# A two-layer hybrid trunk on one core: from the first layer's last tiles through latents and attention, one list of steps in place of the scheduler's order

## The chip, the cores and the metric

One core of a Trainium2 chip runs the whole program in one launch. The time is the device time in microseconds (us), the median of several runs; before the change it is 2141.66 us, from three runs of 2141.5 to 2142.57. One execution is also profiled; its records give every instruction's start and length on the engines: PE (TensorE, matmul and transpose), DVE (VectorE), ACT (ScalarE), POOL (GpSimd) and SP (SyncE, which here issues the loads). Lines such as L170 are lines of the kernel before.

## The reference

The input is a sequence of 1024 tokens by 1024 features in float32. Layer 0 is a gated short convolution with an MLP of 4096, layer 1 is multi-head latent attention with an MLP. Between them a shared key and value side is built from the residual stream. Cut to what this case touches:

```python
def shared_kv(x, c_act, kv_ada_w, kv_ada_b, kv_norm_g, kv_a_w, kv_a_norm_g, kv_b_w, cos, sin):
    ...
    hkv = modulate(rmsnorm(x, kv_norm_g), shift, scale)
    kv_a = hkv @ kv_a_w                                   # 1024 -> 256 + 64
    c_kv = rmsnorm(kv_a[..., :KV_LORA], kv_a_norm_g)
    k_pe = apply_rope(kv_a[..., KV_LORA:], cos, sin)
    kv = (c_kv @ kv_b_w).reshape(B, S, N_HEADS, QK_NOPE + V_HEAD)
    return kv[..., :QK_NOPE], kv[..., QK_NOPE:], k_pe

def mla_mixer(h, q_a_w, q_a_norm_g, q_b_w, o_w, k_nope, v, k_pe, cos, sin):
    q = (rmsnorm(h @ q_a_w, q_a_norm_g) @ q_b_w).reshape(B, S, N_HEADS, QK_NOPE + QK_ROPE)
    ...
    for i in range(S // Q_BLOCK):                         # 8 blocks of 128 queries
        s = q_nope . k_nope + q_pe . k_pe                 # scaled, 8 heads, keys up to the block's end
        s = where(k_chunk <= q_chunk, s, min)             # chunks of 64
        p = softmax(s)
        outs.append(p @ v)
    return concatenate(outs) @ o_w
```

Every layer is wrapped as `x = x + g * rmsnorm(y)`, with shifts, scales and gates that are sums over `silu(c)` times columns of `ada_w`.

## The kernel before

Matrix products are made from two parts of each float32 operand, a high part in a rounded format and the remainder, so that each product is three matmuls (`mm`, L167 to L170). An operand is split by a copy on ACT (L173) and a subtraction on DVE (L174). Token tiles are 128 tokens by 1024 features, and there are eight; feature blocks are 128, and there are eight (`KD`); "halves" are 512 tokens. PSUM is shared by pairs of `mm` and `tp` tiles of one bank and two `big` tiles of two banks.

The stretch that the change touches goes in these steps.

1. *The last rows of the first layer's down projection* (`down`, L889). For each token tile `t` 24 matmuls write a `big` tile, and `Seam.tile` (L298) adds it to `y` (L309), takes the root of the sum of its squares (`squares`, L255 to L257, on ACT), scales it (L315), adds it to the residual tile (L316), stores that, takes its squares too, and at the next tile `flush` writes the normalised tile (L295). For tiles 5 to 7 `front` issues two transposed feature blocks each.
2. *The first products of the query latent* (`first_block`, L632): per feature block three groups of three matmuls, and between them the remaining steps of the transposes (`h_steps`, L475: four transposes L484, an eviction with scale and shift on ACT L486, a split on DVE L490 and L491).
3. *The latents* (`latent`, L1300): for queries (384 features) and keys (256), by halves: copy out of PSUM (L1311), squares (L1312), their sum over features as a product with a matrix of ones (L1315), root (L1316), a reciprocal over 512 columns (L1317), scaling (L1319), a split (L1320, L1321). `rotary_keys` makes the rotated key of 64 features. The second half's steps and the key's steps are issued within the products of the part ahead of them.
4. *Attention* over eight heads. For a head: `keys` (L1424, L1425), `queries` (L1430, L1431), for two heads together `rotary` (L1440, L1441) and `values` (L1454, L1455); then for each of eight blocks of queries, from 7 down to 0, `scores`: five matmuls per 512 keys (L1471), a mask by `memset` (L1472), the maximum (L1474), the exponential with its sum (L1477), and the division (`end`, L1481, L1482). `turn` transposes probabilities (L1497) and splits them (L1500, L1501); `mul` multiplies them by the values; the result is stored (L1532, L1533). The loop over heads gives the program's order: the scores of the next block beside the preparation of the next head and the products of the head before. Loads of a head's weights and five steps of the background sums (`run_bg`, L195, weights by weights) stand at the head's start.

The order in which an engine runs its instructions is fixed when the program is built. Without further words a scheduler chooses it from the program's order and its own estimate of durations. `pinned` (L109) adds edges that make the engines keep the written order for what stands within it. Steps 1 and 2 are pinned in part, attention is not. In the other two places where a down projection meets an up projection, the order of all steps is already a written list, `ORDER` (L45 to L55), which `first_pairs` (L652) follows; its entries are names of steps with their tile or block.

Four `raw` tiles of 512 KB take all loads of weights in turn; a load waits until its tile's last reader is done.

Of the kernel before, what the change touches and what calls it, by code (L numbers as in the profile page):

```python
# [8 lines left out]
F32 = mybir.dt.float32  # L9
# [24 lines left out]
MASKED = -(2.0 ** 127)  # L34
# [17 lines left out]
P5_3 p6_0 nt2d p4_1 p3_2 D9_3 nS2 p6_3 nS3 p7_3 ns2a o6 p4_3 nt3a ns2d p5_3 nt3d o5 o4 p3_3 o3 o7  # L52
""".split()
# [8 lines left out]
def trunk_kernel(ctx: ExitStack, tc: tile.TileContext, x, c, ada_w, ada_b, norm_g, conv_in_w, conv_w,  # L62
# [92 lines left out]
    eps_d = cp.tile([P, 1], F32, name="eps_d")  # L155
    nc.vector.memset(eps_d, D * EPS)
    eps_1 = cp.tile([P, 1], F32, name="eps_1")
    nc.vector.memset(eps_1, EPS)
# [109 lines left out]
    class Seam:  # L268
# [4 lines left out]
        def __init__(self, nx, ys, gmb, xsrc, xdst, last=False):  # L273
            self.nx, self.ys, self.gmb, self.xsrc, self.xdst, self.last = nx, ys, gmb, xsrc, xdst, last
            self.rest, self.backs, self.xr = None, [], {}
# [6 lines left out]
        def front(self, steps, n):  # L282
            for _ in range(min(n, len(steps))):
                f, b = steps.pop(0)
                f()
                self.backs.append(b)

        def back(self):
            while self.backs:
                self.backs.pop(0)()  # L290

        def flush(self):
            if self.rest is not None:
                y, xr, ss = self.rest
                nc.scalar.activation(y, xr, AF.Copy, scale=rroot(ss))  # L295
            self.rest = None

        def tile(self, t, p_, steps):  # L298
# [9 lines left out]
            with pinned():  # L308
                nc.vector.tensor_tensor(y, y, p_, op=ALU.add)  # L309
                self.back()  # L310
                ss = squares(self.nx, y)
                self.flush()
                if t >= 5:
                    self.front(steps, 2)
                nc.vector.scalar_tensor_tensor(y, y, rroot(ss), self.gmb, op0=ALU.mult, op1=ALU.mult)  # L315
                nc.vector.tensor_tensor(xr, xr, y, op=ALU.add)  # L316
                nc.scalar.dma_start(self.xdst[t * P:(t + 1) * P, :], xr)
                if not self.last:
                    self.rest = (y, xr, squares(self.nx, xr))
# [4 lines left out]
        def acts(self, first):  # L324


            acts, ss, sx, rs = {}, {}, {first - 1: self.rest[2]}, {}
# [44 lines left out]
        def finish(self, t, y, xr, p_):  # L372
# [3 lines left out]
            ss, rt, eps = [small(), small()], small(), small()  # L376
            with pinned():
# [3 lines left out]
                nc.vector.tensor_tensor(eps, eps_d, ss[0], op=ALU.add)  # L381
                for sl in halves_:
                    nc.vector.tensor_tensor(self.gmb[:, sl], self.gmb[:, sl], y[:, sl], op=ALU.mult)
                nc.scalar.activation(rt, ss[1], AF.Sqrt, bias=eps)
# [89 lines left out]

    def h_steps(tp, ys, half, key, dst):  # L475

        hi, lo = dst
        s1, sh = vtile["s" + key], vtile["h" + key]
        tts = {}

        def step(k):
            p_ = tp_ps()
            for t in range(4):
                nc.tensor.transpose(p_[:, t * P:(t + 1) * P], ys[half * 4 + t][:, k * P:(k + 1) * P], ident)  # L484
            tt = tp.tile([P, HALF], F32, tag="tt", name=nm("tt"), bufs=2)
            nc.scalar.activation(tt, p_, AF.Identity, scale=s1[:, k:k + 1], bias=sh[:, k:k + 1])  # L486
            tts[k] = tt

        def split(k):
            nc.vector.tensor_copy(hi[:, k, :], tts[k])  # L490
            nc.vector.tensor_tensor(lo[:, k, :], tts[k], hi[:, k, :].bitcast(F32), op=ALU.subtract)  # L491

        return [(lambda k=k: step(k), lambda k=k: split(k)) for k in range(KD)]
# [137 lines left out]

    def first_block(seam, steps0, steps1, ws, h):  # L632

        ps_ = [mm_ps(), mm_ps(), big_ps()[:, :HALF]]
        for k in range(KD):
            with pinned():
                for p_, w in zip(ps_, ws):
                    mm(p_, (w[0][:, k, :], w[1][:, k, :]), (h[0][:, k, :], h[1][:, k, :]), k == 0, k == KD - 1)
                if k == 0:
# [1036 lines left out]
```

## Time and profile before

| | us |
|---|---|
| median of three runs | 2141.66 |
| the profiled execution | 2144.59 |
| its span, first to last instruction | 2142.8 |
| list's stretch: product of tile 5 to the last product of attention | 1004.9 to 1420.5 |
| of it up to the last latent | 1004.9 to 1117.0 |
| of it attention | 1117.0 to 1420.5 |

The granted clock of TensorE is 0.996 on average. Rows of the stretches give busy time of each engine, with the number of instructions in brackets. In the rows of the timeline stand start, length, engine, line, operation and tiles, with the idle time ahead of it and what ended that in square brackets. Rows "A <- B: total, times, longest" say how long A's engine stood idle until B. Rows of groups have "busy, mean ns | idle before". Two matmuls in a row overlap in their records, since a record lasts until its result is written.

### The profile page before, as it was taken

The numbers are of one execution on the slowest core, as the hardware profiler recorded it, in microseconds if no ns is written. First come the engines' busy times: TensorE is split into PE (matmuls) and PEld (weight loads), VectorE is DVE, ScalarE is ACT, GpSimd is POOL, SyncE is SP. The second block draws the span as 40 slices with busy tenths as digits, with TensorE's granted clock in tenths as the row PEclk, the third lists the DMA queues.
The fourth block names the chain that finished last, engine by engine and source line by source line (L and its number), as shares of the span: only waits on it lengthen the run. The fifth ranks groups of instructions, "written<-read, shape, count | busy, mean of one in ns | idle before, by whom it ended". The sixth has DMA issues, their size and how long they took to land.

```text
span 2142.8 us, 25254 instructions
## 1 busy us (share of the span) xinstructions
PE 2083.0 (97%) x9638; PEld 1715.1 (80%) x9638; DVE 1532.3 (72%) x2066; ACT 1060.5 (49%) x1512; POOL 4.0 (0%) x8
## 2 busy tenths in 40 slices
PE   5999999999999999999899999999999999999998
PEld 4888888888888878888777878877888888888887
DVE  5877776977665668876788877766977665558556
ACT  4533353845444434344665555564845444444342
POOL 0000000000000000000000000000000000000000
PEclk9999999999999999999999999999999999999999
DMA  8344454466443976465214231043455543853343
GB/s 245 95 147 146 131 200 136 133 192 215 157 152 131 326 230 226 151 210 178 81 59 124 78 106 44 26 149 132 129 184 184 183 166 134 300 191 122 98 147 138
DMA packets 242336, 330.85 MB, mean 154 GB/s; under 512 B 18630, under 2 KB 143907, under 8 KB 242215
## 3 DMA queue, kind: packets, MB, share of 16 engines
q1 hardware_dynamic: 204328, 248.57, 37.2%
q10 hardware_dynamic: 37886, 80.67, 10.0%
q8 instruction: 76, 1.25, 0.2%
q14 instruction: 46, 0.37, 0.0%
HBM read 248.45 MB, written 80.74 MB: 154 GB/s over the span
## 4 chain that ended last, share of the span: by engine, by line
PE 75%; DVE 12%; ACT 6%; DMA 5%; issue 2%; ACTq 0%; SPq 0%; DVEq 0%
PE one L170 40%; PE mm L170 19%; PE tp L170 7%; PE big L170 3%; ACT junk L255 2%; DMA raw<-in_ada_w_dram 2%; PE big L1471 2%; DVE y L315 1%; DVE raw L316 1%; DVE acc L195 1%; PE tp L1497 1%; DVE small L1474 1%; DVE y L309 1%; DVE pt L1501 1%; ACT small L257 1%
## 5 line engine op out<-in xcount | busy, mean ns | idle before, releaser
L170 PE MATMUL one<-slot,uphi 128*128 128x512 f32 x1240 | 381.9, 389 | 0.0
L170 PEld LDWEIGHTS one<-slot,uphi 128*128 128x128 f32 x1240 | 232.8, 188 | 48.7 <-issue 0.5
L170 PE MATMUL big<-slot 128*128 128x512 f32 x1152 | 267.6, 392 | 0.9 <-DVE slot L174 0.6
L170 PEld LDWEIGHTS big<-slot 128*128 128x128 f32 x1152 | 216.0, 189 | 47.7 <-ACT y L924 1.0
L170 PE MATMUL one<-slot,uplo 128*128 128x512 f32 x620 | 243.0, 392 | 1.6 <-DVE y L584 1.6
L173 ACT ACTIVATE ring<-w 128x1024 fp32r<-128x1024 f32 x98 | 103.8, 1059 | 267.1 <-PE tp L170 145.7
L170 PE MATMUL one<-ring,ring 128*128 128x512 f32 x1008 | 229.5, 389 | 0.3 <-DVE ring L174 0.3
L170 PEld LDWEIGHTS one<-ring,ring 128*128 128x128 f32 x1008 | 189.2, 188 | 40.0 <-DVE ring L174 0.7
L174 DVE TENSOR_TENSOR ring<-w,ring 128x1024 fp32r<-128x1024 f32 x98 | 119.8, 1222 | 122.8 <-ACT ring L173 122.6
L174 DVE TENSOR_TENSOR uplo<-raw,uphi 128x1024 fp32r<-128x1024 f32 x117 | 142.7, 1222 | 79.1 <-ACT uphi L173 79.0
L173 ACT ACTIVATE uphi<-raw 128x1024 fp32r<-128x1024 f32 x117 | 123.7, 1059 | 136.1 <-PE one L170 77.4
L170 PE MATMUL mm<-ring,ring 128*128 128x512 f32 x672 | 163.1, 391 | 2.4 <-DVE ring L174 2.4
L170 PE MATMUL tp<-ring,ring 128*128 128x512 f32 x672 | 161.8, 389 | 0.0
L170 PE MATMUL mm<-slot,uphi 128*128 128x512 f32 x504 | 157.9, 394 | 0.5 <-DVE slot L430 0.5
L170 PEld LDWEIGHTS mm<-ring,ring 128*128 128x128 f32 x672 | 125.6, 188 | 29.7 <-DVE ring L174 3.5
L170 PEld LDWEIGHTS tp<-ring,ring 128*128 128x128 f32 x672 | 126.1, 188 | 26.2
L170 PEld LDWEIGHTS one<-slot,uplo 128*128 128x128 f32 x620 | 116.4, 188 | 26.5 <-DVE y L584 2.4
L195 DVE SCALAR_TENSOR_TENSOR acc<-raw,csil,acc 128x1024 f32<-128x1024 f32 x88 | 112.4, 1277 | 35.1 <-DMA raw<-in_ada_w_dram 32.5
L174 DVE TENSOR_TENSOR ring<-raw,ring 128x1024 fp32r<-128x1024 f32 x98 | 119.3, 1218 | 10.7 <-ACT ring L173 10.7
L170 PE MATMUL one<-slot,s 128*128 128x512 f32 x468 | 114.0, 393 | 0.7 <-DVE s L174 0.7
L170 PEld LDWEIGHTS mm<-slot,uphi 128*128 128x128 f32 x504 | 94.8, 189 | 21.1 <-issue 1.4
L582 ACT ACTIVATE y<-one 128x512 f32<-128x512 f32 x62 | 36.7, 592 | 143.5 <-PE one L170 114.3
(272 smaller groups left out, 3487.0 us busy)
## 6 DMA issues: line engine op xcount, KB each, us to landing
ha<-y ACTq DMA_DIRECT2D x196, 256.0 KB, 3.0
raw<-ha SPq DMA_DIRECT2D x98, 512.0 KB, 4.3
raw<-in_ada_w_dram SPq DMA_DIRECT2D x80, 512.0 KB, 4.4
raw<-in_mlp_up_w_dram SPq DMA_DIRECT2D x70, 512.0 KB, 4.9
w<-in_mlp_down_w_dram SPq DMA_DIRECT2D x56, 512.0 KB, 4.8
raw<-hd SPq DMA_DIRECT2D x24, 512.0 KB, 4.3
xs<-raw ACTq DMA_DIRECT2D x24, 512.0 KB, 3.1
raw<-xs SPq DMA_DIRECT2D x24, 512.0 KB, 4.2
```

Source lines behind the costliest of these rows:

```text
L170: nc.tensor.matmul(out_, lhs[a], rhs[b], start=first and i == 0, stop=last and i == 2, skip_group_check=more)
L173: nc.scalar.activation(hi, src, AF.Copy)
L174: nc.vector.tensor_tensor(lo, src, hi.bitcast(F32), op=ALU.subtract)
L195: nc.vector.scalar_tensor_tensor(acc, raw, s, acc, op0=ALU.mult, op1=ALU.add)
L255: nc.scalar.activation(junk, src, AF.Square, accum_out=ss)
L257: nc.scalar.activation(rt, ss, AF.Sqrt, bias=eps_d)
L309: nc.vector.tensor_tensor(y, y, p_, op=ALU.add)
L315: nc.vector.scalar_tensor_tensor(y, y, rroot(ss), self.gmb, op0=ALU.mult, op1=ALU.mult)
L316: nc.vector.tensor_tensor(xr, xr, y, op=ALU.add)
L582: nc.scalar.activation(dst, x_, AF.Copy)
L1471: nc.tensor.matmul(o_, a, m_, start=j == 0, stop=j == 4)
L1474: nc.vector.tensor_reduce(mx, sp[:, :n], AX.X, ALU.max, negate=True)
```

## The change

A second list, `ATTENTION`, of 1121 entries names every step from the product of tile 5 (`mm5`) to the last output of head 7 (`o7.0`). A letter or two stand for the kind of step, then head (or pair of heads), half, and block. Its first part (up to the first entry that belongs to attention, `bB0`) runs in a pinned context over the engines, the rest in a pinned context over the engines and one over SP, which holds the loads `lq` (query weights), `lk` (key and value weights) and `bl` (rows for background sums). Steps that were one function become several entries: `scores` is `S` (matmuls), `m` (mask and maximum), `e` (exponential), `t` (division); `turn` and `mul` are `T`, `u`, `w` and `P`; keys `K`, `Ka`, `Kd`; and so on.

Beside the order these things change:

- The query latent isn't normalised. Its high part is a scaled copy straight from PSUM, and its squares' sums go, by token, through four matmuls of one column into a column `rsq` for each tile of tokens, `(root of 192 * mean square + eps)` and its reciprocal on eight columns. `rsq` is the scale of the exponential, and the maximum is multiplied by it: one more DVE instruction of one column for each score tile. The scale by 1/sqrt(192) goes with it, so queries' and rotary steps lose their constant factor.
- The key latent's sums go by token too, and its reciprocal root is spread over partitions by four transposes for each half.
- In `Seam.tile` the addition to the residual tile, its store and its squares move from their own tile to the next one, under the wait for that tile's squares. This holds for all three projections that are followed by another one; the last one keeps its order.
- `MASKED` becomes -(2^120). The functions `front`, `back`, `h_steps`, `first_block`, `latent`, `rotated`, `Values` and the loop over heads go.

```diff
+ATTENTION = """
+mm5 tr0_0 tr0_1 add5 tu0_0 mm6 tu0_1 sq5 sp0_1 stt5 rc4 xad5 pre4 mm7 add6 sqx5 sp0_0 sq6 rc5 pre5 stt6 dma5 xad6 tr0_2
+tr0_3 tu0_2 f0 add7 tu0_3 sqx6 sp0_2 tr0_4 mul7 tr0_5 sq7 f1 sp0_3 tu0_5 stt7 dma6 tr0_6 tu0_4 f2 sp0_4 sqx7 rc6 sp0_5 tr0_7
+pre6 f3 rc7 dma7 pre7 tu0_6 f4 tu0_7 sp0_6 sp0_7 tr1_0 tr1_1 tu1_0 f5 tu1_1 sp1_0 sp1_1 tr1_2 tr1_3 tu1_2 f6 tu1_3 sp1_2
...
+Kd2.1 P0.0.1 t1.3 m1.6 P0.0.2 Q2.1 o0.0 Rl1.1.1 e1.6 bs0.6 S1.2 Qa2.1 t1.6 Q2.0 Qd2.1 m1.2 bs0.7 T1.1.0 e1.2 T1.1.1 Qa2.0
+V1.3 t1.2 u1.1.1 Qd2.0 u1.1.0 w1.1.1 S1.0 Va1.3 w1.1.0 K2.0 lq3 m1.0 Vd1.3 e1.0 T1.1.2 Ka2.0 T1.1.3 t1.0 u1.1.2 P1.1.0 Kd2.0
+u1.1.3 P1.1.1 w1.1.2 w1.1.3 V1.1 T1.1.4 Va1.1 P1.1.2 u1.1.4 Vd1.1 P1.1.3 w1.1.4 S2.4 P1.1.4 m2.4 T1.1.5 T1.1.6 S1.1 u1.1.5
...
+P7.1.3 e7.0 w7.1.5 T7.1.6 t7.0 P7.1.4 u7.1.6 T7.0.0 w7.1.6 P7.1.5 u7.0.0 T7.0.1 w7.0.0 P7.1.6 u7.0.1 T7.0.2 P7.0.0 o7.1
+w7.0.1 u7.0.2 P7.0.1 w7.0.2 P7.0.2 o7.0
+""".split()
...
         def flush(self):
             if self.rest is not None:
-                y, xr, ss = self.rest
-                nc.scalar.activation(y, xr, AF.Copy, scale=rroot(ss))
+                t, y, xr = self.rest
+                nc.vector.tensor_tensor(xr, xr, y, op=ALU.add)
+                nc.scalar.dma_start(self.xdst[t * P:(t + 1) * P, :], xr)
+                self.ss = None if self.last else squares(self.nx, xr)
+
+        def tail(self):
+            if self.rest is not None and not self.last:
+                t, y, xr = self.rest
+                nc.scalar.activation(y, xr, AF.Copy, scale=rroot(self.ss))
             self.rest = None
...
                 nc.vector.tensor_tensor(y, y, p_, op=ALU.add)
-                self.back()
                 ss = squares(self.nx, y)
+                if not self.last:
+                    self.flush()
+                nc.vector.scalar_tensor_tensor(y, y, rroot(ss), self.gmb, op0=ALU.mult, op1=ALU.mult)
+                self.tail()
+                self.rest = (t, y, xr)
+                if self.last:
+                    self.flush()
...
+        def token_sums(p_, sq):
+            for t in range(4):
+                nc.tensor.matmul(p_[:, t:t + 1], sq[:, t * P:(t + 1) * P], ones[:, 0:1], start=True, stop=True)
...
+        def k_spread(hf):
+            for t in range(4):
+                nc.tensor.transpose(t_["vs", hf][:, HALF + t * P:HALF + (t + 1) * P], t_["vr", hf][:, t:t + 1].to_broadcast([P, P]), ident)
...
+        def maxima(h, i):
+            n = (i + 1) * P
+            sp, mx = ps_["S", h, i], small()
+            nc.vector.memset(sp[:CHUNK, n - CHUNK:n], MASKED)
+            nc.vector.tensor_reduce(mx, sp[:, :n], AX.X, ALU.max, negate=True)
+            nc.vector.tensor_tensor(mx, mx, rsq[:, i:i + 1], op=ALU.mult)
+            stats[h, i] = mx
+
+        def exponentials(h, i):
...
+            nc.scalar.activation(pts[h, i], ps_.pop(("S", h, i))[:, :n], AF.Exp, scale=rsq[:, i:i + 1], bias=stats[h, i], accum_out=l_)
...
+    with pinned():
+        for name in ATTENTION[:n]:
+            acts[name]()
...
+    attention(acts, t_["qw"], t_["kw"])
+    with pinned(), pinned([mybir.EngineType.SP]):
+        for name in ATTENTION[n:]:
+            acts[name]()
```

776 lines of the change are left out of this document (440 added, 336 removed).

## The prediction

> **What bounds the kernel now.** I read the page's head, then busy time by stretch, then the timeline of TensorE (PE) inside the stretch that the change rewrites, then who waits for whom there.
>
> ```profile
> span 2142.8 us, 25254 instructions
> PE 2083.0 (97%) x9638; PEld 1715.1 (80%) x9638; DVE 1532.3 (72%) x2066; ACT 1060.5 (49%) x1512; POOL 4.0 (0%) x8
> ```
>
> PE bounds the whole. But "busy" hides waits: a matmul's record is longer than the distance to the next one, so a short wait vanishes in the overlap. The distances between starts show the true price.
>
> ```profile
> 943.00 2.88 PE L170 MATMUL mm<-ring,ring 128*128 128x512 f32 x12
> 945.72 2.88 PE L170 MATMUL tp<-ring,ring 128*128 128x512 f32 x12
> ...
> 1390.68 0.34 PE L1471 MATMUL big<-slot,r 128*128 128x384 f32 x1
> 1390.86 0.34 PE L1471 MATMUL big<-k,q 128*128 128x384 f32 x1
> ...
> 1394.93 0.28 PE L1471 MATMUL big<-slot,r 128*128 128x256 f32 x1
> 1395.05 0.28 PE L1471 MATMUL big<-k,q 128*128 128x256 f32 x1
> ...
> 1396.74 0.28 PE L1471 MATMUL big<-k,q 128*128 128x128 f32 x1
> 1396.85 0.27 PE L1471 MATMUL big<-slot,r 128*128 128x128 f32 x1
> ```
>
> Twelve matmuls of 512 columns take 2.72 us from start to start: 0.227 each. 384 columns cost 0.18, 256 cost 0.12, 128 cost 0.11. I use 0.11 for one column too, and about 0.5 per record for the f32 products with `ones`.
>
> ```profile
> 1004.90:1117.00 112.10, 105.18 (x500) 83.46 (x501) 87.61 (x124) 70.90 (x115) 0.00 (x0) 0.98 0.25 81
> 1117.00:1420.50 303.50, 289.67 (x1605) 239.72 (x1604) 238.86 (x476) 171.58 (x340) 0.96 (x1) 0.99 0.25 78
> 1115.00:1157.00 42.00, 36.88 (x188) 29.47 (x187) 40.32 (x63) 25.72 (x44) 0.96 (x1) 1.00 0.43 132
> 1224.80:1299.20 74.40, 71.50 (x408) 60.11 (x406) 59.53 (x120) 41.18 (x84) 0.00 (x0) 1.00 0.27 86
> 1299.20:1371.50 72.30, 70.95 (x408) 59.93 (x406) 51.59 (x111) 41.13 (x84) 0.00 (x0) 1.00 0.11 37
> ```
>
> (Columns: stretch, its length, then PE, weight loads, DVE, ACT, POOL busy with counts, PE clock, DMA share, GB/s.) The first row runs from the product of tile 5 of the first layer's down projection, the list's first entry, to the last latent; the second is attention; then come attention's start and two pairs of heads.
>
> PE's own work follows from the code's counts. Latents: 72 matmuls for tiles 5 to 7, 144 for queries, 96 and 48 for keys and values and the rotary key, all of 512 columns: 360 x 0.227 = 81.7; 128 transposes x 0.11 = 14.1; 8 `ones` records x 0.5 = 4.0. Together 99.8, so 12.3 of 112.1 us is excess. Attention: 696 of 512 columns (K 96, Q 144, rotary 72, scores 240, values' products 144) 158.0; 128 of 384 23.0; 320 of 256 38.4; 416 of 128 45.8; 32 one-column records 3.5; 4 `ones` records 2.0; and 11 of the next projection 2.5. Together 273.2 and 1607 matmuls, beside x1605 in the row. Excess 30.3. **What the change can win is these 42.6 us**, 10% of a stretch in which PE calls itself 95% busy. DVE is the second bound: 239 of 303.5 in attention (79%), 96% in its first 42 us.
>
> **The change part by part.** (a) *The hand-over from the down projection to the latents.* The old order issues two steps of eight transposes behind tiles 5 to 7 and waits:
>
> ```profile
> 1027.05 1.93 PE L484 MATMUL tp<-cs,y 128*128 128x128 f32 x8 [3.39 <-ACT tt L486]
> ...
> 1033.07 1.33 PE L484 MATMUL tp<-cs,y 128*128 128x128 f32 x8 [1.23 <-ACT tt L486]
> 1023.70:1027.10 3.40, 0.05 (x1) 0.05 (x1) 3.29 (x7) 3.25 (x6) 0.00 (x0) 1.00 0.29 116
> 1027.10:1030.50 3.40, 3.40 (x13) 3.01 (x14) 3.33 (x6) 2.79 (x5) 0.00 (x0) 0.50 0.85 260
> ```
>
> 3.39 + 1.23 us of idle, and 3.40 us at a granted clock of 0.50, which loses 1.7: 6.3. The new list interleaves single tiles (`mm6 tu0_1 sq5 ...`) and places five products `f0` to `f4` and their transposes between `mm7` and `tr1_0`: 5 x 9 x 0.227 + 6 x 4 x 0.11 = 12.9 us of PE work over the tail's chain. That chain, priced below: add 1.21, squares 1.5, 0.16, product 1.28, squares 1.5, 0.16, copy 1.14 = 7.0. So it is covered. The second layer already has such a list at the same place, and its waits are what remains:
>
> ```profile
> 1497.09 0.77 PE L418 MATMUL tp<-cs,y 128*128 128x128 f32 x5 [1.72 <-ACT y L295]
> ...
> 1512.77 0.50 PE L170 MATMUL mm<-slot,uplo 128*128 128x512 f32 x1 [0.88 <-DVE slot L429]
> ```
>
> The 1.72 belongs to (d); 0.88 is left, and I allow 1.3. **-5.0** (bounds -6.3, if nothing is left, and -2, if the waits return elsewhere). The half clock goes with its wait. The Trainium skill (TensorE: Matmul & The Clock Gate, Part 1) has the clock halved after an idle window of about 3.4 us. The first drop agrees: it follows 3.40 us with 0.05 busy. The drop at 1412.8 below does not: 2.04 of the 3.40 us ahead of it were busy. By the page no slow stretch would remain; by the rows the second may.
>
> (b) *The rest of the latents.* Four reciprocals over 512 columns go, and queries are no longer normalised: their factor becomes the scale of the exponential.
>
> ```profile
> L1317 DVE RECIPROCAL sq<-sq 128x512 f32<-128x512 f32 x4 | 13.4, 3352 | 5.9 <-ACT sq L1316 5.9
> L1481 DVE RECIPROCAL small<-small 128x1 f32<-128x1 f32 x32 | 5.1, 158 | 8.6 <-ACT p L1477 8.3
> L214 PE MATMUL mm<-ones,acc 128*128 128x1 f32 x32 | 3.7, 245 | 0.0
> ```
>
> DVE loses 13.4 us and gains four of 0.16. Most of it lay beside PE's products, so I count only what PE waited for. PE's sums by token replace the `ones` sums: 16 of them, two records each at 0.11 = 3.5, and 8 transposes spread the keys' root, 0.9: 4.4 against 4.0, so +0.4. Of the 12.3 excess 6.0 is not in (a); I take half away: 0.4 - 3.0 = **-2.6** (bounds -5.6 and +0.4).
>
> (c) *Attention.* The same matmuls, each engine in the listed order. Added are 64 multiplies of one column on DVE between maximum and exponential. Bounds: the reciprocal's 0.16 each, 10 in all, or what an independent small operation delays its successor:
>
> ```profile
> 1149.35 0.11 DVE L1472 MEMSET big<- 64x64 f32 x1
> 1149.38 0.62 DVE L1482 TENSOR_SCALAR p<-p,small 128x768 f32<-128x768 f32 x1
> ```
>
> 0.03, 2 in all. I take 0.15 = 9.6, since this multiply waits for its maximum. DVE's load becomes 238.9 + 9.6 = 248.5. The Trainium skill (VectorE: DVE Perf Modes, The DRAIN you can't avoid) says that the next operation waits until the pipe is empty and advises fewer operations; by it the full price stands, while these two rows, 0.03 apart, show that an independent one does not wait.
>
> What ends PE's waits now is the chain through one score tile:
>
> ```profile
> ACT pt L1500 <- PE tp L1497: 43.2, 42, 3.2
> ACT p L1477 <- DVE small L1474: 34.7, 27, 2.2
> PEld mm L170 <- DVE pt L1501: 9.1, 22, 1.3
> DVE acc L195 <- DMA raw<-in_ada_w_dram: 2.5, 3, 1.7
> ```
>
> The list holds two score tiles in flight and puts other matmuls into each distance. Between `T1.1.1` and `P1.1.0` stand `V1.3`, `S1.0`, `K2.0`, `T1.1.2` and `T1.1.3`: 1.4 + 0.6 + 1.4 + 0.9 = 4.3 us of PE work, over two evictions of 0.6 on ACT and 0.69 on DVE. At the end `S7.0` runs beside head 7's values instead of being held up:
>
> ```profile
> 1408.71 2.00 ACT L173 ACTIVATE slot<-raw 128x1024 fp32r<-128x1024 f32 x2
> ...
> 1411.81 0.37 ACT L1477 ACTIVATE p<-big,small 128x128 f32<-128x128 f32 x1
> 1409.40:1412.80 3.40, 2.04 (x11) 1.30 (x10) 3.26 (x8) 3.40 (x8) 0.00 (x0) 1.00 0.20 43
> 1412.80:1416.20 3.40, 3.40 (x9) 2.62 (x10) 2.40 (x3) 0.90 (x1) 0.00 (x0) 0.50 0.87 292
> ```
>
> There ACT split the next projection's rows ahead of the last exponential. Those splits overwrite slots that the last scores read, and they are not in the list, so part of this hand-over stays. Loads: the queue keeps the list too. A load waiting for one of four `raw` buffers holds back the weights behind it; now such waits cost DVE 2.5 us in three cases at a DMA share of 0.25. I cost the spreading at nothing, since the loads stand many entries ahead of their use; without that cover it is up to 1.7 each.
>
> For the residue I take the second layer's list, quoted in (a): from its first wait to the end of its second 0.88 + 1.72 us of idle stand in 16 us, 16%, but one wait of the two comes from (d); without it 5.5%. Attention has a hand-over at either end and eight even heads between; I take 6% of 273.2 = 16.4 instead of 30.3: **-13.9** (bounds: 2.5%, -23.5; DVE deciding, +20). DVE's share would be 248.5 / 289.6 = 86%, between the 80% of the fullest pair above and the 96% of the start.
>
> (d) *The tile loop ahead of the list,* in all three projections that use it:
>
> ```profile
> 1484.18 1.29 DVE L315 SCALAR_TENSOR_TENSOR y<-y,small,gmb 128x1024 f32<-128x1024 f32 x1
> 1485.50 1.22 DVE L316 TENSOR_TENSOR raw<-raw,y 128x1024 f32<-128x1024 f32 x1
> 1486.64 1.21 DVE L309 TENSOR_TENSOR y<-y,big 128x1024 f32<-128x1024 f32 x1
> 1488.51 1.04 ACT L255 ACTIVATE junk<-y 128x1024 bf16<-128x1024 f32 x1
> 1489.88 1.14 ACT L295 ACTIVATE y<-raw,small 128x1024 f32<-128x1024 f32 x1
> 1490.20 1.28 DVE L315 SCALAR_TENSOR_TENSOR y<-y,small,gmb 128x1024 f32<-128x1024 f32 x1
> ```
>
> A tile takes 1490.20 - 1484.18 = 6.02 us of chain against 24 x 0.227 = 5.45 on PE. The residual sum (1.22) moves to the next tile, under its squares on ACT. From the squares' start to the next product the rows show 1490.20 - 1488.51 = 1.69, of which 0.16 is a reciprocal, so squares are 1.5. The new chain is 1.21 + 1.5 + 0.16 + 1.28 + 0.16 = 4.3, so PE decides. The wait of 1.72 shrinks to about 0.4 in the attention output; the convolution's seam, with the same loop, I give 0.3: **-1.6** (bounds 0 and -3).
>
> **The sum**, in the profiled execution's terms: 2144.59 - 5.0 - 2.6 - 13.9 - 1.6 = 2121.5. That execution was 2.9 above the median 2141.66, so I forecast **2119** (own range 2113 to 2125).
>
> **The rivals.** *DVE paces attention (slower).* Every engine keeps the list, so where DVE is late nothing else may go ahead, and the multiplies lengthen its chain. With a, b and d at -9.2, the kernel gets slower once attention exceeds 312.7, that is when DVE's share falls under 248.5 / 312.7 = 79.5%; now it is 79%. At 77% attention takes 322.7: +19.2 - 9.2, so 2152. For it: 96% busy at the start, and 71% (51.59 of 72.30) in a pair without background sums, where DVE waited on others. Against it: the list puts two or more matmul groups over each eviction. The skill's advice on fewer operations points here.
>
> *Half the gain.* DVE reaches 82.5%, just over the fullest pair: 301.2, -2.3; total -11.5: 2130. For it: durations on the chip differ from those of a search, and each difference is waited out in order.
>
> *The list fits.* Attention's residue is 2.5%: -23.3, total -32.5: 2109. For it: the work repeats (408 matmuls in each of the two pairs above), so one good order serves for all heads. Against it: the end and the start have no cover.
>
> *No change.* What the list wins is eaten at DVE's 79.5%: 2142.
>
> **How the numbers follow.** Forecast 0.45, the list fits 0.19, half 0.17, no change 0.06, DVE paces 0.13. The first three are faster by over 0.2% (4.3 us; less can't be told from no change): 0.81; same 0.06; slower 0.13. The range 2104 to 2142 holds the forecast, half, most of the tight case and half of no change, and leaves out about 0.2.
>
> **What would show it.** (a) no idle of 3.4 us and no clock of 0.50 ahead of the latents; (b) no 3.35 us reciprocals; (c) a pair of heads in 69 to 71 us instead of 72 to 74, DVE above 84%, PE's distances tight; (d) tile to tile 5.45 on DVE in the loop. I am wrong if DVE's share stays at 79%, if PE's waits in attention name DVE more often than now, or if a new slow-clock stretch appears at a hand-over.

## The result, and the profile after

The changed kernel takes 2112.9 us (median of four runs, 2111.67 to 2114.14) against 2142.11 for the kernel before on the same chip: a ratio of 0.9866, 95% interval 0.9853 to 0.9879. It is 29.2 us faster, where the forecast of 2119 meant 22.7. The time lies 0.1 us below the forecast's own range (2113 to 2125) and well within the wide one (2104 to 2142).

The head of the page of the changed kernel (whose lines, as L228 or L1653, are its own from here on):

```profile
span 2112.3 us, 25378 instructions
PE 2071.6 (98%) x9670; PEld 1723.4 (82%) x9670; DVE 1527.6 (72%) x2125; ACT 1060.5 (50%) x1506; POOL 4.1 (0%) x8
```

PE's share rises by one point, and the span falls by 30.5 us. The busy time of the stretches, bounded as in the first two rows of the prediction (columns as there):

```profile
999.50:1098.50 99.00, 97.09 (x497) 81.14 (x496) 68.58 (x113) 60.47 (x97) 1.03 (x1) 0.98 0.28 92
1098.50:1392.40 293.90, 287.44 (x1635) 248.66 (x1634) 252.61 (x542) 176.95 (x346) 0.00 (x0) 0.99 0.25 78
```

By these bounds the latents fall from 112.1 to 99.0 us and attention from 303.5 to 293.9. They mislead a little: the list lets attention's first products and the latents' last steps overlap. So from here on the two are bounded by work: "latents" run from the product of tile 5 to the first product of attention, "attention" from there to the last product with values, and the few matmuls that stand on the wrong side of a bound are moved by their distances (0.227 us each for nine rotary matmuls of the old order and for matmuls of the next projection, 0.11 for four transposes of the new one). Expectations that name a length were made without this correction, which is 2.0 us in the old order. "Conv to down" is the stretch ahead, from the convolution's output products to the first layer's down projection; "attention to down" the one behind.

| | forecast | before | after | difference |
|---|---|---|---|---|
| conv to down (d) | | 682.4 | 677.2 | -5.2 |
| latents (a, b) | -7.6 | 111.4 | 105.0 | -6.4 |
| attention (c) | -13.9 | 301.8 | 287.0 | -14.8 |
| attention to down (d) | | 673.6 | 669.4 | -4.1 |
| sum | -23.1 | | | -30.5 |

The two rows of (d) make -9.3, where -1.6 was forecast. That is all of the difference between the profiled executions. In the seams the waits that the prediction quoted (1.72 and 0.88) have no successor: in the list of PE's waits of the changed kernel from 1440 to 1490 us, and again from 295 to 420, there is no row. The tile loop itself, on DVE in the attention output's seam:

```profile
1449.21 1.28 DVE L368 SCALAR_TENSOR_TENSOR y<-y,small,gmb 128x1024 f32<-128x1024 f32 x1
...
1454.65 1.28 DVE L368 SCALAR_TENSOR_TENSOR y<-y,small,gmb 128x1024 f32<-128x1024 f32 x1
...
1460.09 1.28 DVE L368 SCALAR_TENSOR_TENSOR y<-y,small,gmb 128x1024 f32<-128x1024 f32 x1
```

5.44 us from tile to tile, where it was 6.02: PE's own 5.45 decides, as forecast.

The clock is another matter. Three stretches of half clock stand in the list (two before). Each row pair is a stretch and the one ahead of it:

```profile
1068.70:1072.10 3.40, 1.98 (x17) 1.68 (x16) 3.33 (x7) 2.02 (x3) 0.00 (x0) 1.00 0.01 2
1072.10:1075.50 3.40, 3.40 (x12) 2.92 (x12) 3.33 (x8) 2.31 (x5) 1.03 (x1) 0.50 0.00 0
...
1256.40:1259.80 3.40, 3.33 (x24) 2.79 (x23) 3.26 (x6) 0.33 (x1) 0.00 (x0) 1.00 0.00 0
1259.80:1263.20 3.40, 3.40 (x17) 3.40 (x16) 1.97 (x8) 1.89 (x3) 0.00 (x0) 0.50 0.00 0
...
1382.70:1386.10 3.40, 1.81 (x9) 1.04 (x8) 3.40 (x9) 3.23 (x6) 0.00 (x0) 1.00 0.40 154
1386.10:1389.50 3.40, 3.40 (x17) 3.40 (x16) 2.90 (x4) 0.63 (x2) 0.00 (x0) 0.50 0.66 211
```

3.40 us at 0.50 lose 1.7. The last of them is the hand-over that the prediction left in: ACT and DVE split the next projection's rows (L231, L232), which are not in the list, ahead of the last probabilities, as the timeline shows:

```profile
1381.89 1.23 DVE L232 TENSOR_TENSOR slot<-raw,slot 128x1024 fp32r<-128x1024 f32 x1
...
1383.93 0.41 PE L1671 MATMUL tp<-cs,p 128*128 128x128 f32 x2 [0.91 <-DVE pt L1683]
...
1385.72 0.48 PE L228 MATMUL big<-slot 128*128 128x512 f32 x1 [0.68 <-DVE slot L232]
```

Who PE itself waits for in attention, in us, times and longest, before (1098 to 1385 us) and after (same window):

```profile
PE mm L170 <- DVE pt L1501: 2.6, 9, 0.9
PE big L1471 <- ACT p L1477: 1.7, 2, 1.1
PE mm L170 <- ACT pt L1500: 1.6, 6, 0.3
PE tp L1497 <- DVE p L1482: 1.5, 5, 0.4
```

```profile
PE tp L1671 <- DVE pt L1683: 1.8, 4, 0.9
PE big L1639 <- ACT p L1653: 1.0, 2, 0.6
PE mm L228 <- DVE k L1576: 0.9, 2, 0.6
PE big L1639 <- DVE r L1612: 0.8, 1, 0.8
```

The small waits for probabilities (five for DVE's division, six for ACT's eviction) are gone from the head of the list; what is left names DVE more often than ACT, but less often than before (by the full lists 11 times, before 22).

### The profile page after: what moved, and what is told of

Same layout as the page of the kernel before. It is cut to its first block, busy times and chain, and to the rows that moved or that the text cites. A ratio compares the mean times of both kernels' runs of the same rounds, so it can differ in the third digit from the quotient of the medians.

```text
span 2112.3 us, 25378 instructions
## 1 busy us (share of the span) xinstructions
PE 2071.6 (98%) x9670; PEld 1723.4 (82%) x9670; DVE 1527.6 (72%) x2125; ACT 1060.5 (50%) x1506; POOL 4.1 (0%) x8
## 4 chain that ended last, share of the span: by engine, by line
PE 82%; DVE 12%; ACT 3%; DMA 2%; issue 1%; ACTq 0%; SPq 0%; DVEq 0%
PE one L228 42%; PE mm L228 17%; PE big L228 11%; PE tp L228 7%; PE big L1639 2%; DVE small L1645 1%; DVE acc L1762 1%; ACT junk L313 1%; DVE pt L1683 1%; DMA raw<-in_ada_w_dram 1%; DVE p L1659 1%; PE tp L1671 1%; PE tp L1352 1%; DVE y L364 1%; DVE raw L343 0%
## 5 line engine op out<-in xcount | busy, mean ns | idle before, releaser
L228 PE MATMUL one<-slot,uphi 128*128 128x512 f32 x1240 | 382.1, 389 | 0.0
L228 PEld LDWEIGHTS one<-slot,uphi 128*128 128x128 f32 x1240 | 232.8, 188 | 48.8 <-issue 0.5
L228 PE MATMUL big<-slot 128*128 128x512 f32 x1152 | 263.7, 390 | 0.7 <-DVE slot L232 0.7
L228 PEld LDWEIGHTS big<-slot 128*128 128x128 f32 x1152 | 215.6, 188 | 45.8 <-ACT pt L1679 1.1
L228 PE MATMUL one<-slot,uplo 128*128 128x512 f32 x620 | 243.1, 392 | 1.6 <-DVE y L619 1.6
L231 ACT ACTIVATE ring<-w 128x1024 fp32r<-128x1024 f32 x98 | 103.8, 1059 | 264.6 <-PE tp L228 145.6
L228 PE MATMUL one<-ring,ring 128*128 128x512 f32 x1008 | 229.1, 389 | 0.0
L228 PEld LDWEIGHTS one<-ring,ring 128*128 128x128 f32 x1008 | 189.2, 188 | 39.3
L232 DVE TENSOR_TENSOR ring<-w,ring 128x1024 fp32r<-128x1024 f32 x98 | 119.8, 1222 | 122.3 <-ACT ring L231 122.0
L232 DVE TENSOR_TENSOR uplo<-raw,uphi 128x1024 fp32r<-128x1024 f32 x114 | 139.2, 1223 | 78.5 <-ACT uphi L231 78.5
L231 ACT ACTIVATE uphi<-raw 128x1024 fp32r<-128x1024 f32 x114 | 120.6, 1059 | 135.8 <-PE one L228 84.0
L228 PE MATMUL mm<-ring,ring 128*128 128x512 f32 x672 | 162.9, 390 | 0.4 <-DVE ring L232 0.4
L228 PE MATMUL tp<-ring,ring 128*128 128x512 f32 x672 | 161.8, 389 | 0.0
L228 PEld LDWEIGHTS mm<-ring,ring 128*128 128x128 f32 x672 | 125.6, 188 | 27.5 <-DVE ring L232 1.2
L228 PEld LDWEIGHTS tp<-ring,ring 128*128 128x128 f32 x672 | 126.1, 188 | 26.2
L228 PEld LDWEIGHTS one<-slot,uplo 128*128 128x128 f32 x620 | 116.4, 188 | 26.6 <-DVE y L619 2.4
L228 PE MATMUL mm<-slot,uphi 128*128 128x512 f32 x424 | 131.9, 392 | 0.0
L232 DVE TENSOR_TENSOR ring<-raw,ring 128x1024 fp32r<-128x1024 f32 x98 | 119.3, 1218 | 10.3 <-ACT ring L231 10.3
L228 PE MATMUL one<-slot,s 128*128 128x512 f32 x468 | 114.2, 393 | 0.5 <-DVE s L232 0.5
L253 DVE SCALAR_TENSOR_TENSOR acc<-raw,csil,acc 128x1024 f32<-128x1024 f32 x66 | 84.5, 1281 | 31.7 <-DMA raw<-in_ada_w_dram 29.6
L228 PEld LDWEIGHTS one<-slot,s 128*128 128x128 f32 x468 | 88.9, 190 | 19.3 <-DVE s L232 0.6
```

The costliest lines, as they stand in the source:

```text
L228: nc.tensor.matmul(out_, lhs[a], rhs[b], start=first and i == 0, stop=last and i == 2, skip_group_check=more)
L231: nc.scalar.activation(hi, src, AF.Copy)
L232: nc.vector.tensor_tensor(lo, src, hi.bitcast(F32), op=ALU.subtract)
L253: nc.vector.scalar_tensor_tensor(acc, raw, s, acc, op0=ALU.mult, op1=ALU.add)
```

## The experiments

All are made from the changed kernel, but for one. In the table the number in brackets counts the stretches of half clock within; to compare lengths, take 1.7 us off for each. One stretch of wide is twice as long as the others and counts as two. The ratio is to the kernel before, measured on the same chip.

| kernel | us | ratio, 95% interval | latents | attention | attention to down |
|---|---|---|---|---|---|
| before | 2142.11 | 1 | 111.4 (1) | 301.8 (1) | 673.6 |
| after | 2112.9 | 0.9866 (0.9853 to 0.9879) | 105.0 (1) | 287.0 (2) | 669.4 |
| old_loop | 2122.73 | 0.992 (0.9905 to 0.9935) | 110.2 (2) | 285.6 (1) | 672.7 |
| loop_alone | 2135.75 | 0.9979 (0.997 to 0.9989) | 111.4 (1) | 302.4 (2) | 669.6 |
| loop_order | 2131.42 | 0.9962 (0.9949 to 0.9975) | 103.6 (0) | 303.4 (0) | 669.5 |
| attention_free | 2110.14 | 0.9865 (0.9849 to 0.9882) | 103.4 (0) | 283.7 (0) | 669.5 |
| two_multiplies | 2121.41 | 0.9907 (0.9891 to 0.9924) | 103.4 (0) | 294.5 (1) | 669.5 |
| no_multiply | 2104.66 | 0.9825 (0.981 to 0.9839) | 105.0 (1) | 276.6 (0) | 669.5 |
| loop_no_multiply | 2128.18 | 0.9941 (0.9924 to 0.9957) | 105.1 (1) | 298.4 (0) | 669.5 |
| wide | 2118.84 | 0.9891 (0.9877 to 0.9906) | 103.4 (0) | 291.1 (3) | 669.8 |
| sums_later | 2114.05 | 0.987 (0.9855 to 0.9884) | 106.9 (1) | 284.1 (0) | 669.6 |
| latents_free | 2116.88 | 0.9885 (0.987 to 0.9899) | 107.5 (1) | 285.6 (1) | 669.6 |
| act_multiply | 2107.54 | 0.9844 (0.9829 to 0.9859) | 103.3 (0) | 280.9 (0) | 669.4 |
| act_multiply_free | 2113.08 | 0.9868 (0.9853 to 0.9883) | 103.4 (0) | 285.0 (0) | 670.4 |

Less 1.7 per stretch, the attention of after, old_loop, attention_free, sums_later and latents_free, whose attention is written in the same order with the same multiplies, is 283.6, 283.9, 283.7, 284.1 and 283.9. So lengths can be read to about half a microsecond.

### The tile loop: undone in the changed kernel, and done alone

old_loop:

```diff
                 ss = squares(self.nx, y)
-                if not self.last:
-                    self.flush()
+                self.tail()
                 nc.vector.scalar_tensor_tensor(y, y, rroot(ss), self.gmb, op0=ALU.mult, op1=ALU.mult)
-                self.tail()
                 self.rest = (t, y, xr)
-                if self.last:
-                    self.flush()
+                self.flush()
```

> The changed kernel with the tile loop of before (the residual sum, its store and its squares back in their own tile). Theory: the loop is worth 2.2 us in the convolution's seam and 3.5 us in the attention output's, which is the sum of the waits that vanished there, so 2112.9 + 5.7 = about 2118.6. Rival, as predicted: the loop is worth 1.6 and the other 4 us outside the list came by chance, 2114.5.

loop_alone, made from the kernel before, in the two seams whose order is a written list there (`late` adds the residual tile, stores it and takes its squares):

```diff
                 nc.vector.tensor_tensor(y, y, p_, op=ALU.add)
+                if steps is None:
+                    ss = squares(self.nx, y)
+                    self.late()
+                    nc.vector.scalar_tensor_tensor(y, y, rroot(ss), self.gmb, op0=ALU.mult, op1=ALU.mult)
+                    self.flush()
+                    self.wait = (t, y, xr)
+                    return
...
+        def late(self):
+            if self.wait is not None:
+                t, y, xr = self.wait
+                nc.vector.tensor_tensor(xr, xr, y, op=ALU.add)
+                nc.scalar.dma_start(self.xdst[t * P:(t + 1) * P, :], xr)
+                self.rest = (y, xr, squares(self.nx, xr))
```

> The kernel before with nothing but the new tile loop, in the two seams that were already lists. Theory: 2142.1 - 5.7 = 2136.4, and the waits of 0.6, 1.0, 0.5 and 0.3 us (first layer) and 1.9, 1.0, 0.5 and 0.3 us (second) are gone. Rival: 2140.5, only the first wait of each seam shrinks.

Alone the loop gives 0.21%, 4.5 us, near what was expected; PE's waits in its two seams (295 to 420 and 1470 to 1515 us) are gone here too, so they were the loop's. Undoing it in the changed kernel costs 0.54% (0.992 against 0.9866), 11.6 us, twice the 5.7 that were expected. "Attention to down" tells the seam's share cleanly: 673.6 and 672.7 with the old loop, 669.4 to 669.8 in eleven of the twelve profiles with the new one, 4 us. "Conv to down" is 681.9 on average in the two profiles with the old loop and 678.9 in the twelve with the new one, 3 us, though the latter lie between 676.5 and 680.6: waits for weights in the down projection, such as this one of the kernel before, come and go between profiles.

```profile
778.84 1.43 PE L170 MATMUL mm<-ring,ring 128*128 128x512 f32 x5 [1.71 <-DVE ring L174]
```

The third seam is the one that the prediction had not counted: with the old loop the latents are 5.2 us longer in the changed kernel (1.7 of it a second stretch of half clock), since the list meets a tail that is late. The timeline and the busy time of old_loop:

```profile
1003.50 5.78 PE L228 MATMUL big<-slot 128*128 128x512 f32 x24 [0.20 <-DVE y L364]
1009.12 0.49 PE L1347 MATMUL tp<-cs,y 128*128 128x128 f32 x3
1012.68 1.23 PE L1347 MATMUL tp<-cs,y 128*128 128x128 f32 x5 [3.07 <-ACT y L350]
```

```profile
1009.40:1012.80 3.40, 0.33 (x3) 0.12 (x2) 1.38 (x4) 3.17 (x7) 0.00 (x0) 1.00 0.36 143
1012.80:1016.20 3.40, 3.40 (x11) 2.90 (x12) 2.66 (x3) 1.40 (x4) 0.00 (x0) 0.51 0.69 239
```

An idle of 3.07 us with half clock behind it: nearly the 3.39 of the kernel before. So part (a) needed the loop, not the list alone.

### Is it the order, or that the engines must keep it?

attention_free gives the scheduler the list as the program's order and pins nothing:

```diff
-    with pinned(), pinned([mybir.EngineType.SP]):
-        for name in ATTENTION[n:]:
-            acts[name]()
+    for name in ATTENTION[n:]:
+        acts[name]()
```

> The changed kernel with the attention part of the list as the program's order only: neither the engines nor the load queue are held to it. Theory (a kept order matters since the scheduler's durations differ from the chip's): 2116 to 2124. Rival (the list as a priority is enough): 2113, within 2 us.

loop_order does the same with the entries in the order of the old loop over heads:

```diff
-    with pinned(), pinned([mybir.EngineType.SP]):
-        for name in ATTENTION[n:]:
-            acts[name]()
+    for name in loop_order():
+        acts[name]()
```

> The changed kernel whose attention steps stand in the order of the old loop over heads and are left to the scheduler; the list for the latents stays. Theory (the order is what wins in attention): it gives back the 12.3 us that attention gained, and some more for the 64 added multiplies, 2125 to 2130. Rival (the smaller work wins, the order little): 2113 to 2116.

Same operations, same scheduler, no half clock in either: 303.4 us of attention in the loop's order, 283.7 in the list's. The order is worth 19.7 us, and with 64 multiplies more the old order's attention comes out longer than it was (303.4 against 300.1, less the half clock). That the engines and the load queue keep the list adds nothing here: 0.9865 free, 0.9866 kept. The scheduler did not hold a good order back; it was never shown one.

Ahead of attention this differs:

```diff
-    with pinned():
-        for name in ATTENTION[:n]:
-            acts[name]()
+    for name in ATTENTION[:n]:
+        acts[name]()
```

> The changed kernel with the latents' part of the list as the program's order only; attention is kept to the list. Theory (the written order wins, keeping it does not matter, as in attention): latents in 103 to 106 us, 2111 to 2115. Rival (in the hand-over many steps are ready at once and the scheduler's choice is worse): latents in 107 to 110, 2116 to 2119.

Free, the latents take 105.8 us against 103.3, each less its half clock, because ACT takes other work ahead of the last rows' normalisation (L414), for which the transposes wait:

```profile
1041.25 0.44 PE L1352 MATMUL tp<-cs,y 128*128 128x128 f32 x2 [2.99 <-ACT y L414]
1042.29 0.44 PE L1352 MATMUL tp<-cs,y 128*128 128x128 f32 x2 [0.60 <-ACT y L414]
1043.48 1.97 PE L1352 MATMUL tp<-cs,y 128*128 128x128 f32 x8 [0.76 <-ACT tt L1358]
```

In total it is 0.19% against the changed kernel, and the two intervals overlap; the waits say more than the ratio. The time, 2116.88 us, and the length, 107.5 with its half clock, are the rival's.

### Does DVE pace attention?

One multiply more in each of the 64 score tiles, or none:

```diff
             nc.vector.tensor_tensor(mx, mx, rsq[:, i:i + 1], op=ALU.mult)
+            nc.vector.tensor_tensor(mx, mx, ones[:, 0:1], op=ALU.mult)
```

> The changed kernel with a second multiply of one column (by a column of ones) behind the first for each of the 64 score tiles. Theory: DVE has 41 us of room in attention's 294, and a listed order puts other matmuls over the chain, so of 64 x 0.16 = 10 us of DVE work 0 to 3 us reach the end: 2113 to 2116. Rival (DVE paces attention): 2120 to 2123.

```diff
-            nc.vector.tensor_tensor(mx, mx, rsq[:, i:i + 1], op=ALU.mult)
...
-            nc.scalar.activation(..., AF.Exp, scale=rsq[:, i:i + 1], bias=stats[h, i], accum_out=l_)
+            nc.scalar.activation(..., AF.Exp, bias=stats[h, i], accum_out=l_)
```

> The changed kernel without the multiply of the maximum and with the exponential's scale 1 in place of the column (the queries' normalisation is left out). Theory: 0 to 3 us faster, 2110 to 2113. Rival (DVE paces attention): 2103.

The same in the loop's order:

> Attention's steps in the order of the old loop, left to the scheduler, and without the 64 multiplies (the queries' normalisation is left out). Theory (in that order DVE waits on others and does not pace, so its work costs little): 1 to 3 us faster than the loop's order with the multiplies, attention in 299 to 301 us, about 2129. Rival (DVE's work costs the same in any order): 8 us faster, attention in 293 to 295, about 2123.

Busy time of the whole of attention (fourth number: DVE), first the kernel before, then after, no_multiply, two_multiplies, loop_order and loop_no_multiply:

```profile
1118.10:1420.50 302.40, 288.57 (x1601) 238.81 (x1600) 237.79 (x475) 170.49 (x339) 0.96 (x1) 0.99 0.25 79
```

```profile
1104.10:1392.30 288.20, 281.74 (x1606) 243.82 (x1606) 251.92 (x541) 174.44 (x342) 0.00 (x0) 0.99 0.25 79
```

```profile
1105.60:1383.70 278.10, 275.70 (x1607) 240.80 (x1607) 241.87 (x477) 168.65 (x342) 0.00 (x0) 1.00 0.26 80
```

```profile
1102.70:1399.50 296.80, 284.03 (x1610) 242.82 (x1610) 261.93 (x605) 174.92 (x342) 0.00 (x0) 0.99 0.25 78
```

```profile
1106.20:1410.60 304.40, 288.96 (x1603) 238.14 (x1603) 237.05 (x537) 176.27 (x337) 0.00 (x0) 1.00 0.22 70
```

```profile
1107.70:1407.10 299.40, 286.79 (x1604) 238.28 (x1603) 234.50 (x473) 169.10 (x337) 0.00 (x0) 1.00 0.23 70
```

Read the fourth number against the length: 87.0% without a multiply, 87.4% with one, 88.3% with two. In these three kernels, which keep the list, DVE's share hardly moves while its busy time goes from 241.87 to 261.93, and the length goes with it. Less the half clock, attention is 276.6, 283.6 and 292.8 us, so the first multiply costs 7.0 us (0.11 each) and the second 9.2 (0.14 each), close to DVE's own time for one; both times the rival came out. In the loop's order the share is 77.9% and 78.3%, and the multiplies cost 303.4 - 298.4 = 5.0 us, between the theory's 1 to 3 and the rival's 8. (These two rows hold less DVE work than the others, since four of the background sums are run outside them.)

That in the list the multiplies cost most of their full time is shown. That DVE's load is the reason is shown for a part alone, since a multiply also lengthens the chain from the maximum to the exponential. In attention_free six of the background sums run ahead of attention, DVE is busy 15 us less in it (82.9%), and it is as long as in the changed kernel:

```profile
1102.30:1387.80 285.50, 279.46 (x1608) 240.91 (x1608) 236.75 (x535) 174.37 (x342) 0.00 (x0) 1.00 0.21 68
```

And act_multiply, below, leaves DVE about as little to do as no_multiply (243.53 and 241.87 us), but its attention is 4.3 us longer (280.9 and 276.6).

The price of one, in the timeline of the changed kernel:

```profile
1190.98 1.22 DVE L1645 TENSOR_REDUCE small<-big 128x1 f32<-128x1024 f32 x1
1192.23 0.16 DVE L1646 TENSOR_TENSOR small<-small,rsq 128x1 f32<-128x1 f32 x1
1192.31 0.68 DVE L1683 TENSOR_TENSOR pt<-tp,pt 128x512 fp32r<-128x512 f32 x1
```

Its own record is 0.16; the next, independent, operation starts 0.08 behind its start.

### The wide reciprocals and the queries' sums

wide puts the four reciprocals over 512 columns back on DVE, where those over columns stand, on tiles that nothing reads afterwards:

```diff
             nc.vector.reciprocal(rsq[:, 4 * hf:4 * hf + 4], rsq[:, 4 * hf:4 * hf + 4])
+            wide = t_["sq", hf][1]
+            nc.vector.reciprocal(wide, wide)
...
             nc.vector.reciprocal(rs, rs)
+            wide = t_["sq", "k", hf][1]
+            nc.vector.reciprocal(wide, wide)
```

> The changed kernel with four reciprocals over 128x512 put back on DVE at the places of the small ones, on tiles that nobody reads afterwards. Theory (as priced in the prediction: this DVE work lay beside PE's products): the latents get 0 to 3 us longer, 2113 to 2116. Rival (the latents' gain came from taking these 13.4 us off DVE): 5 us or more, 2118 to 2126.

The latents do not change (103.4 against 103.3, less the half clock): there the 3.3 us of DVE that each takes lie beside PE's products, as the prediction had it. Attention gets longer (291.1 against 287.0), and the total of 2118.84 is the rival's. The last of the four stands at attention's start, where DVE has no gap:

```profile
1107.68 0.17 DVE L1455 RECIPROCAL small<-small 128x4 f32<-128x4 f32 x1
1107.77 3.32 DVE L1457 RECIPROCAL y<-y 128x512 f32<-128x512 f32 x1
1111.01 0.63 DVE L1480 TENSOR_TENSOR y<-big,ctab 128x512 f32<-128x512 f32 x1
```

PE's wait for the next split key grows from 0.63 to 3.46 us, in the timelines of the changed kernel and of wide:

```profile
1110.99 1.70 PE L228 MATMUL mm<-w,ckT 128*128 128x256 f32 x12 [0.63 <-DVE k L1576]
1114.93 2.93 PE L228 MATMUL mm<-w,ckT 128*128 128x256 f32 x12 [3.46 <-DVE k L1580]
```

From 1113.9 to 1120.7 us a stretch of half clock of double length follows. With the one that comes later the half clock costs wide's attention 5.1 us; less that it is 286.0 us against 283.6, so 2.4 more at the same clock.

sums_later moves the three entries `qs1 qr1 qi1` behind `v01`. The first of them is where PE waits in the changed kernel's latents:

```profile
1071.21 1.09 PE L1406 MATMUL big<-ones,sq 128*128 128x1 f32 x8 [1.42 <-DVE sq L1402]
```

```diff
-spk1_2 tuk1_4 qs1 qwa spk1_4 trk1_6 qr1 v01 vq00 qi1 tuk1_6
+spk1_2 tuk1_4 qwa spk1_4 trk1_6 v01 qs1 qr1 qi1 vq00 tuk1_6
```

> The changed kernel with the second half's token sums (qs1, qr1, qi1) moved behind the product v01 in the list. Theory: PE no longer waits 1.6 us for them, and the stretch of 3.4 us at half clock behind that wait, which followed a window with little streaming, goes too, another 1.7: 2109.6, latents in 101.3 instead of 104.6 us. Rival (the clock drops come from elsewhere, and the wait moves on to the next split): within 1 us of 2112.9.

A miss: no gain (0.987 against 0.9866), latents 1.9 us longer. What the wait had hidden comes into the open, transposes that wait for ACT, in the timeline of sums_later:

```profile
1070.70 0.66 PE L1345 MATMUL tp<-cs,y 128*128 128x128 f32 x4 [1.72 <-ACT tt L1351]
...
1079.17 1.12 PE L1345 MATMUL tp<-cs,y 128*128 128x128 f32 x4 [1.54 <-ACT tt L1351]
```

### A version that is faster than both

The multiplies on DVE cost 7 us, and ACT has room; it waits for DVE in front of 33 of the 64 exponentials, as the waits of the changed kernel in attention say:

```profile
ACT p L1653 <- DVE small L1646: 45.0, 33, 4.1
```

So the multiply goes to ACT, ahead of the exponential:

```diff
-            nc.vector.tensor_tensor(mx, mx, rsq[:, i:i + 1], op=ALU.mult)
...
-            l_ = small()
+            l_, b_ = small(), small()
+            nc.scalar.activation(b_, stats[h, i], AF.Copy, scale=rsq[:, i:i + 1])
+            stats[h, i] = b_
```

> The changed kernel with the multiply of the maximum moved from DVE to ACT (a copy of one column with the column as its scale), everything else as listed. Theory (DVE's work paces attention; taking all 64 multiplies away won 8 us): most of that comes back, though ACT gets 64 x 0.2 = 13 us more with some 110 us of room: 2105 to 2108. Rival (the latency from maximum to exponential paces it, on whichever engine it lies): 2112 to 2115.

act_multiply_free is the same with attention not pinned, as in attention_free.

> The same with the attention part of the list as the program's order only. Theory: as the kept one within 2 us, 2104 to 2108, since leaving the list free cost nothing before. Rival (the scheduler's durations mislead it once ACT has more in the chain): 3 us or more slower than the kept one.

act_multiply takes 2107.54 us (2106.89 to 2109.58), 5.4 under the changed kernel, whose runs do not overlap with these (2111.67 to 2114.14); the intervals of the two ratios overlap a little. Its attention is 2.7 us shorter at the same clock, and no stretch of half clock is left in its list. Those three stretches are 5.1 us of the 7.2 between the two profiled executions, and no run shows that they went because of the multiply. DVE is down to 243.53 us and ACT up to 191.29, in the row of its attention:

```profile
1103.00:1386.30 283.30, 278.56 (x1611) 241.44 (x1612) 243.53 (x477) 191.29 (x406) 0.00 (x0) 1.00 0.26 82
```

In the groups of its attention the scaling stands so:

```profile
L1652 ACT ACTIVATE small<-small,rsq 128x1 f32<-128x1 f32 x64 | 18.8, 294 | 39.5 <-DVE small L1645 38.0 <-ACT o L1699 1.2
```

It takes 0.29 us on ACT against 0.16 on DVE, but ACT's wait for DVE at this place falls from 45.0 to 38.0 us. So of the 7.0 us that the multiplies cost, 2.7 come back when they leave DVE, less than the "most" that was expected, though the total fell into its range. The other 4.3 go only when the multiplies go; whether they are the chain, as the rival had it, or ACT's own added time, no run separates. Here keeping the list pays: free, attention is 4.1 us longer and the ratio 0.9868.

## Why the prediction was right, and where it was not

*(a) and (b), the latents: -7.6 forecast, -6.4 measured.* The wait of 3.39 us at the first transposes is gone, and no reciprocal over 512 columns is left. But "so it is covered" held only by the new tile loop: without it (old_loop) the latents win 1.3 us instead of 6.4. The list and the smaller work alone give 3.0 at the same clock, less than the 7.6 that were put down to them, so that the sum came near its forecast is in part luck. That the reciprocals lay beside PE's products was right for the latents (wide), and wrong for the one that runs into attention, which costs 2.4 us there at the same clock and a longer stretch of half clock behind it.

*(c), attention: -13.9 forecast, -14.8 measured.* The residue was sized well, and DVE's share too: 86% forecast, 87.4% measured (251.92 of 288.2). Pairs of heads, from the first product with values to that two heads on, take 71.1, 71.6 and 69.9 us (from 1142.48 to 1355.08 us in all), where they took 72.7, 74.4 and 72.3; 69 to 71 had been named, and the second of the new ones holds a stretch of half clock. An estimate of where the gain lies takes PE's own work by the prediction's prices from each part: what is left falls from 7.7 to 2.7 us ahead of the first product with values, from 16.0 to 10.3 in the three pairs, and from 8.4 to 4.3 behind them. The reason was half right. The order carries it (19.7 us between loop_order and attention_free); that every engine and the queue keep it carries nothing. Hence the argument that durations are "waited out in order" did not bite, and spreading the loads cost nothing, as forecast.

*The multiplies.* 0.15 each was taken from bounds of 0.03 and 0.16. They add 64 times 0.16 of busy time, and 0.11 to 0.14 each of time to the end. The rival "DVE paces attention" was wrong in its sign, since DVE's share rose to 87% where it needed to fall under 79.5% to make the kernel slower. It was right that the multiplies reach the end: 7.0 us were lost to them, 2.7 of which are shown to go when DVE is relieved. The prediction sets its two rows, 0.03 us apart, against the Trainium skill (VectorE: DVE Perf Modes, The DRAIN you can't avoid); that section goes on to say that a next operation which is not held starts earlier. The rows agree with that, and so does the 0.08 above.

*(d), the tile loop: the step that failed.* "The wait of 1.72 shrinks to about 0.4 in the attention output; the convolution's seam, with the same loop, I give 0.3: -1.6 (bounds 0 and -3)." The mechanism was right, tile to tile 5.44 instead of 6.02, but the term was mis-sized by 7.7 us: -9.3 in the two seams by the profiles, 4.1 and 3.0 of it the loop's by the profiles of all runs (7.1 in all; the medians of loop_alone show 4.5), most of the rest waits for weights that came and went. Three things were missed. The wait goes to nothing, not to 0.4. The later waits of the seam (the 0.88 behind DVE's split and two smaller ones) were the same lag, passed on from tile to tile, and went with the first. And the lag also stood at the third seam, the latents' own, where it had been counted as the list's gain.

*The clock.* "The half clock goes with its wait" failed. It went from the hand-over to the latents, but the list holds three stretches, 5.1 us in all, where there were two. The one at 1386 us is at the hand-over behind attention, which had one before (1412.8) and which the prediction left in; those at 1072 and 1260 us are new, inside the latents and inside attention. So the sign that was named for being wrong came, but in other places; each stretch cost 1.7 us.

## What to carry to other kernels

Where a chain behind a tile is longer than the tile's matmuls (6.02 us against 5.45), its lag grows with every tile and is paid at every later wait of the seam, so it is to be priced as the sum of these and not as the first of them. Before engines are pinned to an order, give the order alone to the scheduler; here it was worth 19.7 us by itself, and pinning paid in two places only, 2.5 us in the latents and 4.1 us in attention with the multiply on ACT. An operation on one column can cost most of its full time though matmuls stand beside it: price it by taking it out and by doubling it (7.0 and 9.2 us for 64 here). Then move it to another engine; what comes back (2.7 us here, net of that engine's own added time) is the part of the engine that lost it, and a busy share that stays the same (87%) doesn't tell load from chain.

## What the runs showed of the hardware

The clock falls to half behind windows in which PE is far from idle. Ahead of 1072.1, 1259.8 and 1386.1 us PE was busy for 1.98, 3.33 and 1.81 of 3.40 us. The starts of these stretches lie 187.7 and 126.3 us apart, 55 and 37 times 3.41. Busy time alone does not decide: in the kernel before, a window of the same length, eleven times 3.41 us behind the start of the half clock at 1027.1, has only 1.57 us busy and the full clock behind it:

```profile
1064.70:1068.10 3.40, 1.57 (x9) 1.35 (x10) 2.69 (x5) 3.40 (x7) 0.00 (x0) 1.00 0.72 139
1068.10:1071.50 3.40, 3.40 (x23) 2.87 (x22) 3.26 (x6) 2.29 (x4) 0.00 (x0) 1.00 0.70 261
```

In the window ahead of 1259.8 most records are products of one column; groups of PE in it, in the changed kernel:

```profile
L1771 PE MATMUL mm<-ones,acc 128*128 128x1 f32 x16 | 1.9, 251 | 0.1
L228 PE MATMUL mm<-pt,v 128*128 128x512 f32 x3 | 0.8, 389 | 0.0
```

By distances between starts the wide matmuls there fill some 1.6 of the 3.40 us, the rest is these sixteen. The Trainium skill (TensorE: Matmul & The Clock Gate, Part 1) speaks of an idle window of about 3.4 us; the length agrees with these rows, and that the window must be idle does not. Columns streamed don't decide either: the matmuls of the three windows have 1544, 3856 and 3456 columns, and those of the window at 1064.7 only 3072. What decides stays open; no run tested it by itself, and kernels with the same order of the latents show the stretch at 1072 us in some profiles and not in others.
